# Two split matmuls per unit, and the q/k weights 128 bytes further on

## The chip, the cores and the metric

The kernel runs on one core of one Trainium2 chip. The metric is the device time of one execution in microseconds (us), as the median of several runs. The time of the kernel before is 1561.7 us, the median of three runs.

## The reference, cut to what matters

One decoder layer over a sequence of 512 tokens with model width 2048, all in float32:

```python
xn = _rmsnorm(h, norm_w)
proj = jnp.einsum('bsd,de->bse', xn, w_in)
q, k, v_m, o_m, z_m, i_pre, f_pre, u_g, v_g, z_g = _split_cols(proj)
qk = silu(_causal_depthwise_conv(concat([q, k]), conv_w, conv_b))
hm = _mlstm_chunkwise(q, k, v, log_i, log_f)          # 8 heads, causal
y_m = rmsnorm_per_head(hm) * mlstm_norm_w * sigmoid(o_m) * silu(z_m)
vg = layernorm(gelu(v_g)); sv = einsum('hts,bnshc->bnthc', w_s, vg) + b_spatial
y_g = gelu(u_g) * sv * silu(z_g)
h = h + einsum('bse,ed->bsd', concat([y_m, y_g]), w_out)
return _rmsnorm(h, final_norm_w)
```

Almost all of the arithmetic is the two large products: 512 x 2048 by 2048 x 14352, and 512 x 4096 by 4096 x 2048.

## The kernel before, in words

**Arithmetic.** Each float32 operand is split in two parts of the matmul type float32r: a high part `h`, made by ScalarE as a cast (lines 176 and 186), and the remainder `l`, made by VectorE as a subtraction (lines 177 and 187). A product is the sum of three matmuls, high by high, high by low and low by high. A matmul instruction consists of a weight load of 128 columns (the profile's engine PEld) and the pass of the moving operand (the profile's engine PE).

**Units and chunks.** The input projection is cut in 28 units in a fixed order (`unit_order`, line 40). The first is done with plain products of 512 columns. Each of the other 27 runs through 8 chunks of the contraction and uses a Strassen-like scheme with 7 products in place of 8 (`PRODUCTS`, line 32; `products`, line 785). So a chunk has 7 products x 2 halves t x 3 matmuls = 42 matmuls of 256 columns, and a unit 336. Of each chunk 5 blocks of weights are loaded (640 KB, queue of SyncE, line 150), a second DMA on GpSimd's queue adds two of them in place (line 151), and lines 183 to 187 form the sums and split all 7 blocks into `wh` and `wl`. Chunk n is multiplied while chunk n + 2 is split and chunk n + 4 is loaded (lines 806 to 808). There are three buffers each for `wh` and `wl`, and four for the raw weights `wf`.

**Two kinds of units.** In most units ("token units": vv, oz, uz, v) the stationary operand is a slice of 128 tokens of x, and the moving operand a block of 256 weight columns. In the four units qk the roles are swapped (line 794): the stationary operand is a weight slice, the moving one is x.

**After a unit**, `combine` (line 367) adds the seven accumulators with ScalarE and VectorE, and the rest of the unit's work (activations, the mixing matmul of line 455, the transposes of line 473, the convolution of q and k) is put into a queue `bg`, from which three pieces are taken after each chunk (line 814). So in the third and fourth chunk of the unit behind a uz unit, two groups of four matmuls of line 455 and two groups of four transposes of line 473 stand among the 42 matmuls of a chunk.

**The second half** of the kernel is the output projection. Its part "g" uses plain products of 512 columns (lines 853 to 855), with the eight mLSTM heads in the background, from a shared pool `tp` of twelve temporary buffers of 2 KB. Its part "m" uses `products` again, 4 column groups of 6 chunks (line 876), always in the token roles. A last part does the remaining rows with lines 917 to 919 and the final norm.

**Placement.** The pools stand one behind another in each partition of the on-chip memory, in the order of lines 54 to 61. `gap` and `gap2` hold only spacers, of `GAP_X` and `GAP_W` float32 elements (lines 105 and 106), so they set the byte offset between the pool `xa` (x, 16 buffers of 3072 bytes), `xb` (more of x, 16 buffers of 4096 bytes) and `wp` (the weights). Weights of plain products stand `OFF` = 16 elements (64 bytes) into their buffers (lines 155 and 174); those of all Strassen units stand at offset 0 (lines 180 and 181).

Of the kernel before, what the change touches and what calls it, by code (L numbers as in the profile page):

```python
# [16 lines left out]
P = 128  # L17
D = 2048
S = 512
H = 256  # L20
# [12 lines left out]
    ("q1", 0, 1), ("q6", 4, 5), ("q2", 1, 0), ("q7", 3, 4), ("q5", 6, 3), ("q4", 2, 6), ("q3", 5, 2),  # L33
]
WS = 7 * H
OFF = 16
GAP_X, GAP_W = 24, 112


def unit_order():  # L40
# [7 lines left out]
def hybrid_layer(ctx, tc, xs, x, w_first, w_mid, w_gate, w_out, w_last, par, bif, ws_t, sgu, fin_w, out):  # L48
# [30 lines left out]
    for w in range(9):  # L79
# [13 lines left out]
    nc.gpsimd.memset(ones, 1.0)  # L93
    mhalf = one.tile([P, 8], F32, name="mhalf")
    nc.gpsimd.memset(mhalf, -0.5)
    mask = one.tile([P, P], F32, name="mask")
    nc.gpsimd.memset(mask, 0.0)
    nc.gpsimd.affine_select(
        out=mask, in_=mask, pattern=[[1, P]], compare_op=ALU.is_ge,
        fill=BIG, base=0, channel_multiplier=-1,  # L100
    )
    r_tok = one.tile([P, NT], F32, name="r_tok")
    r_b = one.tile([P, S], F32, name="r_b")
    gst = one.tile([P, 14, NH], F32, name="gst")
# [14 lines left out]
    chunks = []  # L119
    for un in range(NA):  # L120
        for j in range(NP):
            chunks.append(("std", w_first[j]) if un == 0 else ("str", w_mid[un - 1, j]))
    NB0 = len(chunks)
    b_chunks = []
    for kind in "gm":
# [26 lines left out]

    def split_first(a):
        if 0 not in splits:
            splits[0] = tuple(wp.tile([P, WS], F32R, tag=tag, name=f"{tag}0", bufs=3)[:, OFF:OFF + 1024].rearrange(
                "p (a b) -> p a b", a=2) for tag in ("wh", "wl"))
        h, l = splits[0]
        f = raws[0][:, a * S:(a + 1) * S]
        nc.scalar.copy(h[:, a, :], f)
        nc.vector.tensor_tensor(l[:, a, :], f, h[:, a, :].bitcast(F32), op=ALU.subtract)  # L160

    def split(n):
        if n >= NCH or n in splits:
            return
        kind = chunks[n][0]
        t = raws[n]
        raws[n] = None
        if kind == "std":
            if n >= NF0 + 2:
                h = xb.tile([P, 2, S], F32R, tag="xb", name=f"fh{n}")  # L170
                l = xb.tile([P, 2, S], F32R, tag="xb", name=f"fl{n}")
            else:
                h, l = (wp.tile([P, WS], F32R, tag=tag, name=f"{tag}{n}", bufs=bufs)[
                    :, OFF:OFF + 1024].rearrange("p (a b) -> p a b", a=2) for tag, bufs in (("wh", 3), ("wl", 3)))
            f = t[:, 0:1024].rearrange("p (a b) -> p a b", a=2)
            nc.scalar.copy(h, f)  # L176
            nc.vector.tensor_tensor(l, f, h.bitcast(F32), op=ALU.subtract)  # L177
            splits[n] = (h, l)
            return
        h = wp.tile([P, WS], F32R, tag="wh", name=f"wh{n}", bufs=3)  # L180
        l = wp.tile([P, WS], F32R, tag="wl", name=f"wl{n}", bufs=3)
        e = wp.tile([P, 2 * H], F32, tag="we", name=f"we{n}", bufs=1)
        nc.vector.tensor_tensor(e[:, 0:H], t[:, 3 * H:4 * H], t[:, 2 * H:3 * H], op=ALU.add)  # L183
        nc.vector.tensor_tensor(e[:, H:2 * H], e[:, 0:H], t[:, 0:H], op=ALU.add)  # L184
        for f, c in ((t, slice(0, 5 * H)), (e, slice(5 * H, WS))):
            nc.scalar.copy(h[:, c], f)  # L186
            nc.vector.tensor_tensor(l[:, c], f, h[:, c].bitcast(F32), op=ALU.subtract)  # L187
        splits[n] = tuple(v.rearrange("p (a b) -> p a b", a=7) for v in (h, l))
# [58 lines left out]
            nc.scalar.activation(t, t, AF.Square, accum_out=ssq8[:, tt, c:c + 1])  # L247

    def stats_end():
        ssq = sm.tile([P, NT], F32, tag="s4", name="ssq", bufs=8)  # L250
        nc.vector.reduce_sum(ssq, ssq8, axis=mybir.AxisListType.X)
        nc.vector.tensor_scalar(ssq, ssq, 1.0 / D, EPS, op0=ALU.mult, op1=ALU.add)
        nc.gpsimd.tensor_tensor(r_tok, ssq, mhalf[:, :NT], op=ALU.pow)
# [307 lines left out]
    def st_s(h, s0):  # L561
        w = S - s0 * P
        (qh, ql), (kh, kl) = qk_t[h]
        ks = slice(s0 * P, (s0 + 1) * P)
        wm = max(w, H)
        ps_ = bank(f"s{h}_{s0}")
        nc.tensor.matmul(ps_[:, 0:wm], lhsT=kh[:, ks], rhs=qh[:, S - wm:], start=True, stop=False)
        nc.tensor.matmul(ps_[:, 0:wm], lhsT=kh[:, ks], rhs=ql[:, S - wm:], start=False, stop=False)
        nc.tensor.matmul(ps_[:, 0:wm], lhsT=kl[:, ks], rhs=qh[:, S - wm:], start=False, stop=True)
        ps = ps_[:, wm - w:wm]  # L570
        pt = temp(f"p{h}_{s0}")
        cb = cb_t[h]
        g = gst[:, pair(s0, s0), h:h + 1]
        nc.vector.scalar_tensor_tensor(pt[:, 0:P], in0=cb[:, s0 * P:(s0 + 1) * P], scalar=g, in1=mask,
                                       op0=ALU.subtract, op1=ALU.max)
        nc.scalar.activation(pt[:, 0:P], pt[:, 0:P], AF.Exp, scale=-1.0)
        for t0 in range(s0 + 1, NT):
            nc.scalar.activation(pt[:, (t0 - s0) * P:(t0 - s0 + 1) * P], cb[:, t0 * P:(t0 + 1) * P], AF.Exp,
                                 scale=-1.0, bias=gst[:, pair(s0, t0), h:h + 1])
        nc.vector.scalar_tensor_tensor(pt[:, 0:w], in0=ps[:, 0:w], scalar=float(P) ** -0.5, in1=pt[:, 0:w],  # L580
                                       op0=ALU.mult, op1=ALU.mult)
        if s0 == 0:
            hi, lo = (xa.tile([P, 3 * H], F32R, tag="xa", name=f"s{c}{h}_0")[:, 0:S] for c in "hl")
        elif s0 == 1:
            t = xa.tile([P, 3 * H], F32R, tag="xa", name=f"s{h}_1")
            hi, lo = t[:, 0:w], t[:, w:2 * w]
        else:
            if s0 == 2:
                sp_t[(h, "t")] = xa.tile([P, 3 * H], F32R, tag="xa", name=f"s{h}_2")
            t = sp_t[(h, "t")][:, (0 if s0 == 2 else 512):]  # L590
            hi, lo = t[:, 0:w], t[:, w:2 * w]
        nc.scalar.copy(hi, pt[:, 0:w])
        nc.vector.tensor_tensor(lo, pt[:, 0:w], hi.bitcast(F32), op=ALU.subtract)
        sp_t[(h, s0)] = (hi, lo)
# [17 lines left out]
    def st_norm(h):  # L612
        oz_t[h] = []
        for a in range(2):
            t = half(f"oz{h}_{a}")
            nc.gpsimd.dma_start(t, oz_dram[h][:, 2 * a:2 * a + 2, :])
            oz_t[h].append(t)
        ht = h_t[h]
        da = sm.tile([P, NT], F32, tag="s4", name=f"da{h}", bufs=8)
        nc.vector.scalar_tensor_tensor(da, in0=den_t[h], scalar=-1.0, in1=den_t[h], op0=ALU.mult, op1=ALU.max)  # L620
        nc.vector.tensor_tensor(da, da, gst[:, 10:14, h], op=ALU.max)
        rr = sm.tile([P, NT], F32, tag="s4", name=f"rr{h}", bufs=8)
        nc.vector.reciprocal(rr, da)
        ssq = sm.tile([P, NT], F32, tag="s4", name=f"sq{h}", bufs=8)
        junk = temp(f"jk{h}")[:, 0:H]
        for t0 in range(NT):
            nc.scalar.activation(junk, ht[t0 // 2][:, t0 % 2, 0:H], AF.Square, scale=rr[:, t0:t0 + 1],
                                 accum_out=ssq[:, t0:t0 + 1])
        nc.vector.tensor_scalar(ssq, ssq, 1.0 / H, EPS, op0=ALU.mult, op1=ALU.add)
        rn = sm.tile([P, NT], F32, tag="s4", name=f"rn{h}", bufs=8)  # L630
        nc.gpsimd.tensor_tensor(rn, ssq, mhalf[:, :NT], op=ALU.pow)
        hc = sm.tile([P, NT], F32, tag="hc", name=f"hc{h}", bufs=4)
        nc.vector.tensor_tensor(hc, rr, rn, op=ALU.mult)
        hc_t[h] = hc
# [83 lines left out]
        while tag not in done:  # L718
            bg.popleft()()

    act_warm = sm.tile([P, 8], F32, tag="aw", name="act_warm", bufs=1)
    nc.scalar.copy(act_warm, mhalf)

    load_x(0)
# [57 lines left out]
        return {name: (pp if p < 4 else pm).tile([P, S], F32, tag="p" if p < 4 else "m", name=f"{name}_{un}")  # L782
                for p, (name, _, _) in enumerate(PRODUCTS)}

    def products(q, xj, wh, wl, opening, closing, features):
        for name, xsl, wsl in PRODUCTS:
            xh, xl = xj[xsl]
            ps = q[name]
            for t in range(2):
                o = ps[:, t * H:(t + 1) * H]  # L790
                cs = slice(t * P, (t + 1) * P)
                first, last = opening and t == 0, closing and t == 1
                if features:
# [1 line left out]
                else:  # L795
                    ops = ((xh[:, cs], wh[:, wsl, :]), (xh[:, cs], wl[:, wsl, :]), (xl[:, cs], wh[:, wsl, :]))
                for a, (st_, mv_) in enumerate(ops):
                    nc.tensor.matmul(o, lhsT=st_, rhs=mv_, start=(first and a == 0), stop=(last and a == 2),  # L798
                                     skip_group_check=True)

    for un in range(1, NA):
        kind, i = order[un]
        q = product_banks(un)
        for j in range(NP):
            n = un * NP + j
            load(n + 4)
            split(n + 2)
            products(q, X[j], *splits.pop(n), j == 0, j == NP - 1, kind == "qk")
            if j == NP - 1:
                c = combine(un, q)  # L810
                AFTER[kind](i, c)
            if un == NA - 1 and j >= 1:
                load_y("g", j - 1)
            run_bg(3)
    while bg:
        run_bg(1)
    load_y("g", NP - 1)
    bg.append(gates)
    queue_loads(0)
    bg.extend([pause] * 6)  # L820
    bg.append(gate_shifts)
# [13 lines left out]
    for m, (kind, dq, g) in enumerate(b_chunks):  # L835
# [31 lines left out]
        else:  # L867
            if g == 0:
                q = product_banks(f"m{dq}")
                res = {}  # L870
                for a in range(2):
                    for b in range(2):
                        t = half(f"xc{dq}_{a}{b}")
                        nc.sync.dma_start(t, block(acc_dram, a, b, dq))
                        res[(a, b)] = t
            products(q, Y[("m", g)], wh, wl, g == 0, g == 5, False)
            if g == 5:
                c = combine(f"m{dq}", q)
                for a in range(2):
# [142 lines left out]
```

## Time and profile before

| | |
|---|---|
| median of 3 runs | 1561.7 us (1553.22 to 1561.98) |
| profiled execution, its own time | 1571.57 us |
| span of the profiled execution, first to last instruction | 1569.9 us |
| mean granted TensorE clock | 0.997 |
| matmuls / weight loads | 11864 / 11864 |

The profile is one execution recorded by the hardware. A row of the timeline gives the start of an instruction in us from the span's start, its duration, engine, line of the kernel, output and inputs by name, and shape. A duration there includes a pipeline latency, so matmuls overlap in it: how fast they follow one another is read from the differences of their starts. A row of the table of windows gives a stretch of time and, for each engine, its busy time and in brackets how many instructions had a part in the stretch.

### The profile page before, as it was taken

To read this page: it belongs to the slowest core of one execution; us is meant where nothing else is said; L and a number is where in the kernel's file an instruction comes from. 1 tells how busy PE (TensorE), PEld (TensorE's weight loads), DVE (VectorE), ACT (ScalarE), POOL (GpSimd) and SP (SyncE) were. 2 spreads that over 40 slices of the span, in tenths; PEclk is the share of its full clock that TensorE was granted. 3 is DMA by queue.
4 is the path that set the end of the run, shared out by engine and by line. 5 is a ranking of instruction groups with operands and counts; after the bars stand their busy time and mean duration, and the time that the engine had idled before them with its cause. 6 is when DMAs were issued, how large, how long until landed. Compare 5 with 4: busy or idle time off the path is not lost. (4 is left out here: it accounts for less than half of the span.)

```text
span 1569.9 us, 30095 instructions
## 1 busy us (share of the span) xinstructions
PE 1545.9 (98%) x11864; PEld 1485.4 (95%) x11864; DVE 1183.7 (75%) x1944; ACT 874.6 (56%) x1340; POOL 285.3 (18%) x384
## 2 busy tenths in 40 slices
PE   9999999999999999999999999999999999999997
PEld 7899999999999999999999999999988788889986
DVE  8787767877966876976877977678887665697875
ACT  6665455654654555554655565454776666553333
POOL 1411112211122211121211111111202222011100
PEclk9999999999999999999999999999999999999999
DMA  9777878787788777778787777877964665798962
GB/s 319 210 192 187 228 177 209 185 202 193 213 203 215 188 211 184 210 190 214 192 211 186 200 203 199 212 201 196 277 195 156 206 226 188 238 265 238 277 231 107
DMA packets 118510, 326.99 MB, mean 208 GB/s; under 512 B 13534, under 2 KB 20702, under 8 KB 118369
## 3 DMA queue, kind: packets, MB, share of 16 engines
q1 hardware_dynamic: 77456, 243.30, 48.1%
q0 software_dynamic: 40192, 80.66, 26.7%
q8 instruction: 93, 1.52, 0.4%
q10 hardware_dynamic: 720, 1.11, 0.2%
q14 instruction: 49, 0.39, 0.1%
HBM read 229.37 MB, written 32.74 MB: 167 GB/s over the span
## 5 line engine op out<-in xcount | busy, mean ns | idle before, releaser
L186 ACT CAST wh<-wf 128x1280 fp32r<-128x1280 f32 x240 | 301.9, 1264 | 379.9 <-issue 237.8
L187 DVE TENSOR_TENSOR wl<-wf,wh 128x1280 fp32r<-128x1280 f32 x240 | 356.7, 1488 | 174.3 <-ACT wh L186 174.0
L798 PE MATMUL q<-wh,xbh 128*128 128x256 f32 x1472 | 413.7, 281 | 1.4 <-ACT e L774 1.4
L798 PE MATMUL q<-wl,xbh 128*128 128x256 f32 x1472 | 412.9, 281 | 1.2 <-DVE wl L187 1.2
L798 PE MATMUL q<-wh,xbl 128*128 128x256 f32 x1472 | 412.7, 280 | 0.0
L151 POOL DMA_DIRECT2D wf<-wf x240 | 205.3, 857 | 1010.9 <-DMA wf<-w_mid 243.2
L798 PE MATMUL q<-wh,xah 128*128 128x256 f32 x1104 | 311.8, 282 | 0.0
L798 PE MATMUL q<-wl,xah 128*128 128x256 f32 x1104 | 309.5, 280 | 0.0
L798 PE MATMUL q<-wh,xal 128*128 128x256 f32 x1104 | 309.4, 280 | 0.0
L798 PEld LDWEIGHTS q<-wh,xbh 128*128 128x128 f32 x1472 | 281.1, 191 | 1.8 <-ACT e L774 1.6
L798 PEld LDWEIGHTS q<-wl,xbh 128*128 128x128 f32 x1472 | 276.9, 188 | 1.9 <-DVE wl L187 1.8
L798 PEld LDWEIGHTS q<-wh,xbl 128*128 128x128 f32 x1472 | 276.3, 188 | 0.0
L798 PEld LDWEIGHTS q<-wh,xah 128*128 128x128 f32 x1104 | 210.8, 191 | 0.7 <-ACT e L774 0.2
L798 PEld LDWEIGHTS q<-wl,xah 128*128 128x128 f32 x1104 | 207.7, 188 | 0.1
L798 PEld LDWEIGHTS q<-wh,xal 128*128 128x128 f32 x1104 | 207.2, 188 | 0.0
L186 ACT CAST wh<-we 128x512 fp32r<-128x512 f32 x240 | 148.2, 618 | 89.6 <-DVE we L184 89.2
L187 DVE TENSOR_TENSOR wl<-we,wh 128x512 fp32r<-128x512 f32 x240 | 164.7, 686 | 17.2 <-ACT wh L186 17.2
L183 DVE TENSOR_TENSOR we<-wf 128x256 f32<-128x256 f32 x240 | 101.4, 422 | 20.0 <-issue 9.0
L184 DVE TENSOR_TENSOR we<-we,wf 128x256 f32<-128x256 f32 x240 | 101.4, 423 | 5.4
L853 PE MATMUL og<-wh,ygh 128*128 128x512 f32 x256 | 100.9, 396 | 1.6 <-ACT wh L176 1.6
L854 PE MATMUL og<-wl,ygh 128*128 128x512 f32 x256 | 101.5, 397 | 0.1
L855 PE MATMUL og<-wh,ygl 128*128 128x512 f32 x256 | 101.3, 396 | 0.0
(284 smaller groups left out, 2865.9 us busy)
## 6 DMA issues: line engine op xcount, KB each, us to landing
wf<-w_mid SPq DMA_DIRECT2D x216, 640.0 KB, 4.7
wf<-wf POOLq DMA_DIRECT2D x240, 256.0 KB, 5.2
wf<-w_out_p SPq DMA_DIRECT2D x40, 512.0 KB, 4.1
wf<-w_last SPq DMA_DIRECT2D x24, 640.0 KB, 5.7
xr<-xs SPq DMA_DIRECT2D x16, 256.0 KB, 6.1
xt<-x SPq DMA_DIRECT2D x8, 512.0 KB, 7.5
ozd<-e SPq DMA_DIRECT2D x16, 256.0 KB, 2.6
ygd<-yfg SPq DMA_DIRECT2D x16, 256.0 KB, 4.5
```

What stands on the lines that cost most here:

```text
L151: nc.gpsimd.dma_start(t[:, 3 * H:5 * H], t[:, H:3 * H], accum_op=ALU.add)
L183: nc.vector.tensor_tensor(e[:, 0:H], t[:, 3 * H:4 * H], t[:, 2 * H:3 * H], op=ALU.add)
L184: nc.vector.tensor_tensor(e[:, H:2 * H], e[:, 0:H], t[:, 0:H], op=ALU.add)
L186: nc.scalar.copy(h[:, c], f)
L187: nc.vector.tensor_tensor(l[:, c], f, h[:, c].bitcast(F32), op=ALU.subtract)
L798: nc.tensor.matmul(o, lhsT=st_, rhs=mv_, start=(first and a == 0), stop=(last and a == 2), skip_group_check=True)
L853: nc.tensor.matmul(acc[q], lhsT=yh[:, kk, cs], rhs=wh[:, kk, :], start=st, stop=False)
L854: nc.tensor.matmul(acc[q], lhsT=yh[:, kk, cs], rhs=wl[:, kk, :], start=False, stop=False)
L855: nc.tensor.matmul(acc[q], lhsT=yl[:, kk, cs], rhs=wh[:, kk, :], start=False, stop=sp_)
```

## The change

It has three parts.

1. **Two cuts per unit.** In each of the 27 Strassen units, one of the 42 matmuls of chunk 0 (product q3, second half, first of three) and one of chunk 4 (product q1, second half, first of three) is issued as two matmuls of 128 columns, each with the same stationary operand and its own weight load. In the part "m" the same is done in chunks 1 and 3 of each of the four column groups (product q1). That makes 27 x 2 + 4 x 2 = 62 matmuls more. The sums are the same.
2. **Placement.** The weight buffers get 64 elements (256 bytes) longer. In the qk units the weights stand 128 bytes into the buffer (`OFF_FEAT`); in the token units they stay at 0. The spacers shrink from 24 to 16 and from 112 to 48 elements.
3. **Small tiles.** The triangular mask (512 bytes, made at the start) becomes a buffer of the pool `tp`, made by GpSimd at the beginning of part "g" through the queue `bg`, and kept for all heads; small tiles of tag s4 go from 8 to 6 buffers; a scratch tile moves into `tp`.

```diff
 WS = 7 * H
-OFF = 16
-GAP_X, GAP_W = 24, 112
+WSLOT = WS + 64
+OFF, OFF_TOK, OFF_FEAT = 16, 0, 32
+GAP_X, GAP_W = 16, 48
...
-    mask = one.tile([P, P], F32, name="mask")
-    nc.gpsimd.memset(mask, 0.0)
-    nc.gpsimd.affine_select(out=mask, in_=mask, ...)
+    masks = []
+    def make_mask():
+        mask = temp("mask")[:, 0:P]
+        nc.gpsimd.memset(mask, 0.0)
+        nc.gpsimd.affine_select(out=mask, in_=mask, ...)
+        masks.append(mask)
...
-            chunks.append(("std", w_first[j]) if un == 0 else ("str", w_mid[un - 1, j]))
+            chunks.append(("std", w_first[j]) if un == 0 else
+                          ("strf" if order[un][0] == "qk" else "str", w_mid[un - 1, j]))
...
-        h = wp.tile([P, WS], F32R, tag="wh", name=f"wh{n}", bufs=3)
-        l = wp.tile([P, WS], F32R, tag="wl", name=f"wl{n}", bufs=3)
+        o = OFF_FEAT if kind == "strf" else OFF_TOK
+        h, l = (wp.tile([P, WSLOT], F32R, tag=tag, name=f"{tag}{n}", bufs=3)[:, o:o + WS] for tag in ("wh", "wl"))
...
-                    nc.tensor.matmul(o, lhsT=st_, rhs=mv_, start=(first and a == 0), stop=(last and a == 2),
-                                     skip_group_check=True)
+                    parts = (0, P, H) if (name, t, a) == cut else (0, H)
+                    for c0, c1 in zip(parts, parts[1:]):
+                        nc.tensor.matmul(ps[:, t * H + c0:t * H + c1], lhsT=st_, rhs=mv_[:, c0:c1],
+                                         start=(first and a == 0), stop=(last and a == 2), skip_group_check=True)
...
-            products(q, X[j], *splits.pop(n), j == 0, j == NP - 1, kind == "qk")
+            cut = {0: ("q3", 1, 0), 4: ("q1", 1, 0)}.get(j)
+            products(q, X[j], *splits.pop(n), j == 0, j == NP - 1, kind == "qk", cut)
...
     bg.append(gates)
+    bg.append(make_mask)
...
-            products(q, Y[("m", g)], wh, wl, g == 0, g == 5, False)
+            products(q, Y[("m", g)], wh, wl, g == 0, g == 5, False, ("q1", 1, 0) if g in (1, 3) else None)
```

More of the change, by code (lines that the diff above doesn't have):

```diff
@@ L95, in hybrid_layer @@
     nc.gpsimd.memset(mhalf, -0.5)
-    mask = one.tile([P, P], F32, name="mask")
-    nc.gpsimd.memset(mask, 0.0)
[L98 to L101, printed above, removed]
+    masks = []
+    def make_mask():
+        mask = temp("mask")[:, 0:P]
+        nc.gpsimd.memset(mask, 0.0)
+        nc.gpsimd.affine_select(
+            out=mask, in_=mask, pattern=[[1, P]], compare_op=ALU.is_ge,
+            fill=BIG, base=0, channel_multiplier=-1,
+        )
+        masks.append(mask)
     r_tok = one.tile([P, NT], F32, name="r_tok")
@@ L154, in split_first @@
         if 0 not in splits:
-            splits[0] = tuple(wp.tile([P, WS], F32R, tag=tag, name=f"{tag}0", bufs=3)[:, OFF:OFF + 1024].rearrange(
+            splits[0] = tuple(wp.tile([P, WSLOT], F32R, tag=tag, name=f"{tag}0", bufs=3)[:, OFF:OFF + 1024].rearrange(
                 "p (a b) -> p a b", a=2) for tag in ("wh", "wl"))
@@ L172, in split @@
             else:
-                h, l = (wp.tile([P, WS], F32R, tag=tag, name=f"{tag}{n}", bufs=bufs)[
+                h, l = (wp.tile([P, WSLOT], F32R, tag=tag, name=f"{tag}{n}", bufs=bufs)[
                     :, OFF:OFF + 1024].rearrange("p (a b) -> p a b", a=2) for tag, bufs in (("wh", 3), ("wl", 3)))
@@ L249, in stats_end @@
     def stats_end():
-        ssq = sm.tile([P, NT], F32, tag="s4", name="ssq", bufs=8)
+        ssq = sm.tile([P, NT], F32, tag="s4", name="ssq", bufs=6)
         nc.vector.reduce_sum(ssq, ssq8, axis=mybir.AxisListType.X)
@@ L573, in st_s @@
         g = gst[:, pair(s0, s0), h:h + 1]
-        nc.vector.scalar_tensor_tensor(pt[:, 0:P], in0=cb[:, s0 * P:(s0 + 1) * P], scalar=g, in1=mask,
+        nc.vector.scalar_tensor_tensor(pt[:, 0:P], in0=cb[:, s0 * P:(s0 + 1) * P], scalar=g, in1=masks[0],
                                        op0=ALU.subtract, op1=ALU.max)
@@ L618, in st_norm @@
         ht = h_t[h]
-        da = sm.tile([P, NT], F32, tag="s4", name=f"da{h}", bufs=8)
+        da = sm.tile([P, NT], F32, tag="s4", name=f"da{h}", bufs=6)
         nc.vector.scalar_tensor_tensor(da, in0=den_t[h], scalar=-1.0, in1=den_t[h], op0=ALU.mult, op1=ALU.max)
         nc.vector.tensor_tensor(da, da, gst[:, 10:14, h], op=ALU.max)
-        rr = sm.tile([P, NT], F32, tag="s4", name=f"rr{h}", bufs=8)
+        rr = sm.tile([P, NT], F32, tag="s4", name=f"rr{h}", bufs=6)
         nc.vector.reciprocal(rr, da)
-        ssq = sm.tile([P, NT], F32, tag="s4", name=f"sq{h}", bufs=8)
+        ssq = sm.tile([P, NT], F32, tag="s4", name=f"sq{h}", bufs=6)
         junk = temp(f"jk{h}")[:, 0:H]
@@ L629, in st_norm @@
         nc.vector.tensor_scalar(ssq, ssq, 1.0 / H, EPS, op0=ALU.mult, op1=ALU.add)
-        rn = sm.tile([P, NT], F32, tag="s4", name=f"rn{h}", bufs=8)
+        rn = sm.tile([P, NT], F32, tag="s4", name=f"rn{h}", bufs=6)
         nc.gpsimd.tensor_tensor(rn, ssq, mhalf[:, :NT], op=ALU.pow)
@@ L719, in flush @@
             bg.popleft()()
-    act_warm = sm.tile([P, 8], F32, tag="aw", name="act_warm", bufs=1)
+    act_warm = temp("act_warm")[:, 0:8]
     nc.scalar.copy(act_warm, mhalf)
@@ L783, in product_banks, with products @@
                 for p, (name, _, _) in enumerate(PRODUCTS)}
-    def products(q, xj, wh, wl, opening, closing, features):
+    def products(q, xj, wh, wl, opening, closing, features, cut=None):
         for name, xsl, wsl in PRODUCTS:
@@ L789, in products @@
             for t in range(2):
-                o = ps[:, t * H:(t + 1) * H]
                 cs = slice(t * P, (t + 1) * P)
```

## The prediction, made before the changed kernel was run

> **What bounds the kernel now.** I read the page first: the span, the share of each engine, the largest groups.
>
> ```profile
> span 1569.9 us, 30095 instructions
> ...
> PE 1545.9 (98%) x11864; PEld 1485.4 (95%) x11864; DVE 1183.7 (75%) x1944; ACT 874.6 (56%) x1340; POOL 285.3 (18%) x384
> ...
> L798 PE MATMUL q<-wh,xbh 128*128 128x256 f32 x1472 | 413.7, 281 | 1.4 <-ACT e L774 1.4
> L798 PE MATMUL q<-wl,xbh 128*128 128x256 f32 x1472 | 412.9, 281 | 1.2 <-DVE wl L187 1.2
> ```
>
> PE is busy for 98% of the span, and line 798, the Strassen matmul, is most of it: 30 x 336 = 10,080 of the 11,864 matmuls. Next the waits of PE up to 1150 us, and one line of all waits.
>
> ```profile
> PE q L798 <- ACT e L774: 1.4, 1, 1.4
> PE p L760 <- ACT wh L159: 1.3, 1, 1.3
> PE q L798 <- DVE wl L187: 1.2, 3, 0.8
> ```
>
> ```profile
> ACT wh L186 <- PE q L798: 94.5, 46, 3.2
> ```
>
> PE waits for next to nothing. ScalarE waits 94.5 us for PE to give back a weight buffer, so the splits run ahead of PE. Only what PE itself takes per matmul can move the time much. The mean of 281 ns in the page is overlapped and hides that; the starts in the timeline show it. Here are the first and the last row of two stretches, of 161 and 155 matmuls in unbroken sequence:
>
> ```profile
> 389.77 0.28 PE L798 MATMUL q<-wh,xah 128*128 128x256 f32 x1
> ...
> 407.90 0.28 PE L798 MATMUL q<-wl,xah 128*128 128x256 f32 x1
> ```
>
> ```profile
> 1052.78 0.28 PE L798 MATMUL q<-xah,wh 128*128 128x256 f32 x1
> ...
> 1070.91 0.28 PE L798 MATMUL q<-xbl,wh 128*128 128x256 f32 x1
> ```
>
> 18.13 us / 160 = **113.3 ns** in the first, 18.13 / 154 = **117.7 ns** in the second. Instruction, shape and clock are the same; there are two paces, 4.4 ns apart. The table of windows, matmuls of line 798 alone, shows where each holds (the count includes two or three that overlap an edge):
>
> ```profile
> 104.00:144.00 40.00, 40.00 (x342) 1.00 0.75 201
> 630.00:670.00 40.00, 40.00 (x342) 1.00 0.80 214
> 1440.00:1470.00 30.00, 30.00 (x257) 1.00 0.97 272
> 388.60:437.00 48.40, 47.85 (x420) 1.00 0.76 205
> 1073.80:1116.00 42.20, 41.97 (x367) 1.00 0.79 213
> ```
>
> (342 - 2) / 40 us is 117.6 ns, and 117.6 again in the part "m" at 1440. The fast pace holds in the last two windows and in some short stretches. Counted over all starts of line 798, about 1,060 matmuls run at the fast and 8,920 at the slow pace; the rest has a break before or after it. How a stretch becomes fast or slow is in the timeline:
>
> ```profile
> 156.73 0.81 PE L455 MATMUL mx<-e,ws 128*128 128x256 f32 x3
> 157.19 0.47 PE L798 MATMUL q<-wh,xbh 128*128 128x256 f32 x1
> 157.50 0.28 PE L798 MATMUL q<-wl,xbh 128*128 128x256 f32 x1
> 157.62 0.28 PE L798 MATMUL q<-wh,xbl 128*128 128x256 f32 x1
> 157.74 0.28 PE L798 MATMUL q<-wh,xah 128*128 128x256 f32 x1
> ...
> 158.19 0.28 PE L798 MATMUL q<-wl,xah 128*128 128x256 f32 x1
> ```
>
> ```profile
> 161.14 0.66 PE L473 MATMUL ytg<-ident,e 128*128 128x128 f32 x4
> 161.56 0.36 PE L798 MATMUL q<-wh,xah 128*128 128x256 f32 x1
> 161.76 0.28 PE L798 MATMUL q<-wl,xah 128*128 128x256 f32 x1
> ...
> 162.93 0.28 PE L798 MATMUL q<-wh,xbl 128*128 128x256 f32 x1
> ```
>
> After the mixing matmuls four intervals take 0.45 us (113 ns); after the second group of transposes, ten take 1.17 us (117). This repeats in all token units that hold these groups: fast after line 455, slow after the second group of line 473, and then it stays, for up to 1,280 matmuls. So the pace is a phase between weight loads and moving passes: it keeps itself up, and a short foreign instruction can shift it. In the qk units, where the two operands swap places, the same mixing matmuls do not help. First and last of the 18 matmuls between two groups of line 455:
>
> ```profile
> 355.86 1.02 PE L455 MATMUL mx<-e,ws 128*128 128x256 f32 x4
> ...
> 357.78 0.28 PE L798 MATMUL q<-xbh,wh 128*128 128x256 f32 x1
> ...
> 359.79 0.28 PE L798 MATMUL q<-xbh,wl 128*128 128x256 f32 x1
> ```
>
> 2.01 / 17 = 118 ns. No matmul sequence in the four qk units is fast.
>
> **Why the placement can matter.** `xa`, `xb` and the weights consist of buffers and slices that are multiples of 256 bytes. The first weight buffer stands 16 x 3072 + 16 x 4096 + 448 bytes behind the first x buffer, which is 192 modulo 256. So stationary minus moving address is 64 modulo 256 in token units and 192 in qk units. After the change the spacer is 192 instead of 448 bytes: again 192 modulo 256, so token units keep their 64. With 128 bytes more, a qk unit gets 192 + 128 = 64 as well. If the phase depends on this residue, qk units become like token units. That the period is 256 bytes is an assumption; that the swap matters is seen.
>
> **The change part by part**, against the profiled execution's own 1571.57 us, 0.6% above the median of 1561.7.
>
> - *Slow matmuls made fast.* The first cut comes with the last product of chunk 0, when a unit has taken all its accumulators, the second at the start of chunk 4, just behind the last transposes. If each cut leaves the fast phase, as the short groups of line 455 do, 8,920 x (117.7 - 113.3) = **-39.7 us** (4.45 unrounded). Bounds: 0, if a cut leaves the phase as it was, to -39.7.
> - *Left slow.* Chunk 3 behind the transposes up to the second cut, some 34 matmuls in each of eight units, and the starts before the first cuts: 450 x 4.4 ns = **+2.0**.
> - *The cuts themselves.* 62 more weight loads and passes. No row shows a float32r matmul of 128 columns; the nearest is the transposes of 128 columns, four of which take 161.14 to 161.56, 105 ns each. The halves have as many columns together as the whole, so the lower bound is 0; the upper is a whole slow interval, 118 ns. I take 105: **+6.5** (0 to 7.3). TensorE: Matmul & The Clock Gate in the Trainium skill, section LDWEIGHTS, puts a load of 128 columns at 107 ns; by it the term would be an estimated +6.6.
> - *Settling.* The two intervals behind 157.50 are 0.12 instead of 0.113, and with rounding I allow 0.02 us per cut: **+1.2**.
> - *VectorE.* At the fast pace a unit takes 38.1 us in place of 39.6. The heaviest units for VectorE are those behind a qk unit:
>
> ```profile
> 389.00:427.00 38.00, 37.81 (x334) 37.61 (x333) 36.11 (x59) 21.05 (x26) 6.20 (x8) 1.00 0.78 212
> 588.00:629.00 41.00, 40.97 (x342) 40.55 (x342) 28.57 (x41) 22.97 (x30) 6.53 (x8) 1.00 0.73 185
> ```
>
> The first is fast already, with VectorE (fourth column) busy for 36.11 of 38 us, and the other, a typical one, needs 28.57. So VectorE keeps up on the whole, with short waits in seven heavy units, of the size of the three above (1.2 us together, 0.8 the longest): **+2.3** (0 to 5.6).
> - *Part "m"* at 1440 has its DMA engines busy for 0.97 of the time and may not follow a faster pace: its 1,008 matmuls are worth 4.5 us, I take **+1** (0 to 4.5).
> - *Mask in the pool.* Part "g" has 11 instead of 12 buffers for everything else. Its fills are on GpSimd:
>
> ```profile
> L98 POOL TENSOR_SCALAR_AFFINE_SELECT mask<-mask 128x128 f32<-128x128 f32 x1 | 0.5, 497 | 0.0
> ```
>
> ```profile
> 1227.17 1.66 PE L473 MATMUL ytm<-ident,oz 128*128 128x128 f32 x4 [2.51 <-DVE oz L639]
> 1228.48 0.77 PE L853 MATMUL og<-wh,ygh 128*128 128x512 f32 x1
> 1229.06 0.63 PE L854 MATMUL og<-wl,ygh 128*128 128x512 f32 x1
> ```
>
> The fill stands on GpSimd's queue ahead of the first head's DMAs, which are six chunks early; 0.5 us there is hidden. A missing buffer would show as one more wait like that of 2.51 us. I take one, less what is hidden: **+2** (0 to 20, one for each of eight heads). Fewer s4 buffers and the moved scratch tile cost 0: a head uses four s4 tiles and six are left.
>
> Sum: -39.7 + 2.0 + 6.5 + 1.2 + 2.3 + 1 + 2 = **-24.7 us**; 1571.57 - 24.7 = 1546.9 for a profiled execution. Scaled by 1561.7 / 1571.57 that is **1537 us**.
>
> **The rivals.** *Half an effect.* The residue matters modulo 512, not 256. The new weight buffer of 7424 bytes is 14.5 x 512, so every other buffer would stand wrong, or the fast phase does not last from one cut to the next. For it: the phase did flip within units. Against it: it lasted over unit borders (388.6 to 437). Half of the gain with the cuts paid: -19.9 + 6.5 + 1.2 + 2 = -10, 1552 us.
>
> *Nothing happens.* Two cuts and an offset do not shift the phase: +6.5 + 2 = +8.5, 1570 us. For it: the stop of 1.4 us at the first unit ended slow too, so not every disturbance helps. Against it: line 455 always did. SBUF — State Buffer in the Trainium skill, section Who interferes with whom, speaks for this rival: TensorE has independent read ports for moving operand and weight load and never waits for anyone, so an address could not matter. The trace disagrees in part, with 113.3 and 117.7 ns for one instruction; what causes it no row shows.
>
> *The cut sets the slow phase*, as the second group of 128-column transposes always does (161.14). The place is each cut; from the first on, the 1,060 fast matmuls are lost too: 1,060 x 4.45 ns = +4.7, with the cuts +6.5 and the mask +2 it is +13.2, 1575 us, slower. It decides if the interval behind a cut is 118 ns and stays so.
>
> **How the numbers follow.** The forecast has a chance of 0.62, half an effect 0.14, nothing 0.13, slower 0.11. The forecast's own range is 1526 (cuts free, no new waits) to 1549 (qk units stay slow, 4 x 336 x 4.45 ns = 6 us, and more waits on the pool). To leave out no more than 2 in 10, the range must take in half an effect and reach towards nothing with cheap cuts: **1524 to 1567**. A measurement can tell about 1% from no change, that is under 1546 or over 1577. The forecast is below that but for 0.04, half an effect mostly above: faster 0.62, same 0.32, slower 0.06.
>
> **What would show it.** Right: windows of 40 us in the token units hold about 355 matmuls of line 798 in place of 342, those of the qk units too; behind the cut in chunk 4 the interval falls from 118 to 113 ns within some five matmuls; there are 11,926 matmuls. Wrong: 118 ns behind the cuts (then the phase was not theirs to set); fast token units but slow qk units (then the residue isn't the rule); fast pace with the gain lost in waits of PE for `wl` of line 187, for `wf`, or in part "g" for a temporary buffer.

## The result, and the profile after

| | kernel before | changed kernel |
|---|---|---|
| median of 16 runs | 1562.53 us | 1551.95 us |
| lowest to highest | 1553.22 to 1571.74 | 1548.60 to 1559.74 |
| ratio, 95% interval | | 0.9929 (0.9910 to 0.9948) |
| profiled execution, its own time | 1571.57 us | 1551.84 us |

The change makes the kernel faster by 0.7%, 10.6 us, where 24.7 us were forecast. Between the two profiled executions the difference is 19.7 us. These two numbers, 10.6 and 19.7, are the first thing to explain. One run of the changed kernel, in its repetition below, took 3090.84 us, twice the others; its ratio leaves it out, and nothing here shows why. The page of the changed kernel:

```profile
span 1550.1 us, 30205 instructions
...
PE 1522.6 (98%) x11926; PEld 1461.1 (94%) x11926; DVE 1182.3 (76%) x1944; ACT 876.1 (57%) x1340; POOL 279.0 (18%) x384
...
L806 PE MATMUL q<-wh,xbh 128*128 128x256 f32 (+1 forms) x1495 | 409.5, 276 | 1.4 <-ACT e L781 1.4
L806 PE MATMUL q<-wl,xbh 128*128 128x256 f32 x1472 | 409.9, 278 | 1.0 <-DVE wl L194 1.0
```

Line 806 is what line 798 was. PE stays the bound, with 62 instructions more and 23 us less of busy time. The means fell from 281 to 276 and 278 ns. The waits of PE up to 1150 us, and ScalarE's wait for PE:

```profile
PE q L806 <- DVE wl L194: 1.0, 3, 0.3
```

```profile
ACT wh L193 <- PE q L806: 114.0, 50, 3.3
```

So the splits still run ahead. The windows that were read before, for line 806:

```profile
104.00:144.00 40.00, 40.00 (x355) 1.00 0.81 213
630.00:670.00 40.00, 39.55 (x345) 1.00 0.82 211
1440.00:1470.00 30.00, 29.84 (x259) 1.00 0.95 263
```

The first has 355 matmuls where there were 342. The second has 345, since a stop and a group of transposes now fall into it. The third, in part "m", has 259 in place of 257, although 221 of its matmuls run at the fast pace: two cuts and, at the border between two column groups, short stops of 0.8 us together fall into it. And a cut that starts from the slow pace, the second of the first Strassen unit (the row with x2 is the cut matmul):

```profile
85.02 0.28 PE L806 MATMUL q<-wh,xah 128*128 128x256 f32 x1
85.13 0.28 PE L806 MATMUL q<-wl,xah 128*128 128x256 f32 x1
85.25 0.28 PE L806 MATMUL q<-wh,xal 128*128 128x256 f32 x1
85.37 0.33 PE L806 MATMUL q<-wh,xah 128*128 128x128 f32 x2
85.54 0.34 PE L806 MATMUL q<-wl,xah 128*128 128x256 f32 x1
...
86.19 0.28 PE L806 MATMUL q<-wh,xbh 128*128 128x256 f32 x1
...
87.43 0.28 PE L806 MATMUL q<-wh,xbl 128*128 128x256 f32 x1
```

From 86.19 to 87.43 are eleven intervals of 113 ns: slow before the cut, fast behind it. Counted over all starts, 8,394 matmuls of line 806 run at 113.3 and 1,365 at 117.8 ns; in the profile of before it was 1,058 and 8,921. Below, "slow" is this number of matmuls at the slow pace.

### The profile page after: what moved, and what is told of

It is laid out like the page before. It is cut to its first block, busy times and chain, and to the rows that moved or that the text cites. A ratio compares the mean times of both kernels' runs of the same rounds, so it can differ in the third digit from the quotient of the medians.

```text
span 1550.1 us, 30205 instructions
## 1 busy us (share of the span) xinstructions
PE 1522.6 (98%) x11926; PEld 1461.1 (94%) x11926; DVE 1182.3 (76%) x1944; ACT 876.1 (57%) x1340; POOL 279.0 (18%) x384
## 5 line engine op out<-in xcount | busy, mean ns | idle before, releaser
L806 PE MATMUL q<-wh,xbh 128*128 128x256 f32 (+1 forms) x1495 | 409.5, 276 | 1.4 <-ACT e L781 1.4
L806 PE MATMUL q<-wh,xbl 128*128 128x256 f32 x1472 | 407.2, 277 | 0.0
L806 PE MATMUL q<-wh,xah 128*128 128x256 f32 (+1 forms) x1127 | 308.0, 277 | 0.4 <-DVE e L380 0.4
L806 PE MATMUL q<-wh,xal 128*128 128x256 f32 x1104 | 305.4, 277 | 0.0
```

Of the source, the lines that this page charges most:

```text
L806: nc.tensor.matmul(ps[:, t * H + c0:t * H + c1], lhsT=st_, rhs=mv_[:, c0:c1], start=(first and a == 0), stop=(last and a == 2), skip_group ...
```

## The experiments

### The same kernel again

Three more profiles of the kernel before, to see whether the one that was read is typical. No edit.

> The unchanged kernel before, profiled once more. Theory A (the share of fast matmuls differs from execution to execution, and the profile of before on which the prediction was built caught a slow one): this execution's own time lies nearer the median of 1562.5 us, and its number of slow matmuls of line 798 is lower than 8,921 by 225 for each us that it is below 1571.6, so some 6,900 at 1562.5 us. Theory B (profiling itself, or another stage, made those 9 us): about 1571 us again with about 8,920 slow matmuls, or a lower time with the same 8,920.

> The same kernel a third time, for a third point. Theory A: time and number of slow matmuls again lie on one line of 4.4 ns per slow matmul, wherever the time falls. Theory B: no such line.

> The kernel before, profiled a fourth time. Theory A (time follows the share of fast matmuls, which differs from execution to execution): if the time is near the median of 1562 us, 6,000 to 7,500 slow matmuls; near 1553 us, 4,000 to 5,000; near 1571 us, 7,800 to 9,000. It falls if a time under 1556 us comes with over 7,500 slow ones, or one over 1568 us with fewer than 6,000.

| execution of the kernel before | its time | slow in all | slow in the input projection | time of these units |
|---|---|---|---|---|
| the one that the prediction read | 1571.57 us | 8,921 | 7,918 | 1092.6 us |
| second | 1552.32 us | 4,142 | 3,898 | 1077.0 us |
| third | 1571.79 us | 7,848 | 7,618 | 1095.3 us |
| fourth | 1564.52 us | 5,874 | 5,619 | 1085.7 us |

The second execution, in the windows of 104 and 1030 us; the latter lies in the last qk unit:

```profile
104.00:144.00 40.00, 40.00 (x356) 1.00 0.79 204
...
1030.00:1060.00 30.00, 30.00 (x266) 1.00 0.85 222
```

356 matmuls in 40 us and 266 in 30 us are the fast pace, without any cut, and in a qk unit on the old placement too. So the share of fast matmuls differs from one execution to the next, from a tenth to more than half, and the time goes with it. In the units of the input projection (line 798 up to the first matmul of part "g") the four executions lie on one line of 4.4 ns per slow matmul within about 2 us: from 3,898 to 7,918 it would be +17.8 us and was +15.6. Over the whole kernel the line is less clean. The third execution has 1,073 slow matmuls fewer than the first and the same time. Of these, 773 are in part "m", worth 3.4 us, and it became only 1.3 us shorter, since its stops grew from 0.5 to 2.6 us. The fourth has 5,874 where I expected 6,000 or more. Theory B (profiling makes the 9 us) falls with the second execution: profiled, and 1552.32 us.

### Each part of the change alone

The changed kernel without cuts:

```diff
-            cut = {0: ("q3", 1, 0), 4: ("q1", 1, 0)}.get(j)
+            cut = None
...
-            products(q, Y[("m", g)], wh, wl, g == 0, g == 5, False, ("q1", 1, 0) if g in (1, 3) else None)
+            products(q, Y[("m", g)], wh, wl, g == 0, g == 5, False, None)
```

> The changed kernel without any cut, so placement, mask and small tiles alone. Theory A (cuts set the phase, the residue of 64 bytes lets it last): token units as in the kernel before, mostly slow after the second transposes, but the qk units can now be fast, also after line 462's mixing matmuls; some 300 to 1,500 slow matmuls fewer, ratio 0.995 to 1.003. Rival (the placement alone does it): nearly all matmuls fast and a ratio of 0.990 or lower, since the cuts' cost is saved too.

The kernel before with the cuts alone, on the old placement, the mask where it was:

```diff
+                    parts = (0, P, H) if (name, t, a) == cut else (0, H)
+                    for c0, c1 in zip(parts, parts[1:]):
...
+            cut = {0: ("q3", 1, 0), 4: ("q1", 1, 0)}.get(j)
...
```

> The kernel before with the 62 cuts alone, on the old placement. Theory A: token units and the part m fast nearly throughout, the four qk units slow (1,344 matmuls at 118 ns), ratio 0.993 to 0.998: the changed kernel's gain less 4 x 336 x 4.4 ns = 6 us, plus some 3 us if the mask in the pool cost that in part g. Rival (cuts work only with the new placement): token units slow behind the cuts, ratio 1.000 to 1.006.

| | median | ratio to before, interval | slow |
|---|---|---|---|
| placement alone | 1566.06 us | 1.0015 (0.9991 to 1.0038) | 5,502 |
| cuts alone | 1550.26 us | 0.9923 (0.9893 to 0.9953) | 1,589 |
| both (changed kernel) | 1551.95 us | 0.9929 (0.9910 to 0.9948) | 1,365 |

The cuts do all of it. Placement alone is not faster, and its number of slow matmuls is one that the kernel before has too. Its four qk units, which I had expected could be fast now, were slow for 231 to 336 of their 336 matmuls. I had expected the qk units to be slow throughout with cuts alone, and they are not. The first three have 241 slow matmuls each (110 in the changed kernel), and the fourth, in which no transposes stand, has none. So the new placement saves 3 x 131 x 4.4 ns = 1.7 us there, too little to show in the ratios.

### What the residue decides

The changed kernel with the two offsets exchanged, so that stationary minus moving address is 192 modulo 256 in all Strassen units:

```diff
-OFF, OFF_TOK, OFF_FEAT = 16, 0, 32
+OFF, OFF_TOK, OFF_FEAT = 16, 32, 0
```

> The changed kernel with the two offsets exchanged: token weights 128 bytes on, q and k weights at 0, so that stationary minus moving address is 192 modulo 256 in every Strassen unit. Theory C (the residue does not decide whether a fast phase can last, only what a disturbance leaves behind): units without disturbances fast from the first cut on, 1,400 to 3,000 slow matmuls, 1550 to 1558 us. Theory D (64 is needed, as the prediction had it): token units slow behind every cut, over 7,000 slow matmuls, 1570 us or more.

1569.03 us, ratio 1.0017 (0.9994 to 1.0040), 5,775 slow: between what the two theories gave. Its first cut in chunk 0 of the second unit:

```profile
108.83 0.28 PE L806 MATMUL q<-wh,xbh 128*128 128x256 f32 x1
108.95 0.28 PE L806 MATMUL q<-wl,xbh 128*128 128x256 f32 x1
109.07 0.28 PE L806 MATMUL q<-wh,xbl 128*128 128x256 f32 x1
109.19 0.33 PE L806 MATMUL q<-wh,xbh 128*128 128x128 f32 x2
109.36 0.33 PE L806 MATMUL q<-wl,xbh 128*128 128x256 f32 x1
109.53 0.28 PE L806 MATMUL q<-wh,xbl 128*128 128x256 f32 x1
...
110.24 0.28 PE L806 MATMUL q<-wh,xal 128*128 128x256 f32 x1
```

From 109.53 to 110.24 are six intervals of 118 ns: slow before the cut, slow behind it. The same cut in the changed kernel, which comes from the fast pace:

```profile
108.51 0.28 PE L806 MATMUL q<-wh,xbl 128*128 128x256 f32 x1
108.62 0.33 PE L806 MATMUL q<-wh,xbh 128*128 128x128 f32 x2
108.79 0.33 PE L806 MATMUL q<-wl,xbh 128*128 128x256 f32 x1
108.96 0.28 PE L806 MATMUL q<-wh,xbl 128*128 128x256 f32 x1
109.08 0.28 PE L806 MATMUL q<-wh,xah 128*128 128x256 f32 x1
109.20 0.28 PE L806 MATMUL q<-wl,xah 128*128 128x256 f32 x1
109.32 0.28 PE L806 MATMUL q<-wh,xal 128*128 128x256 f32 x1
109.43 0.28 PE L806 MATMUL q<-wh,xah 128*128 128x256 f32 x1
...
109.77 0.28 PE L806 MATMUL q<-wh,xbh 128*128 128x256 f32 x1
```

Here the phase is first pushed (0.12 us each from 108.96 to 109.32) and settles at 113 ns from 109.43 on. In the exchanged kernel a cut from the fast pace is followed by 113 ns at once, and two of the first fourteen cuts did turn a slow stretch fast; the others left what they found. Counted over all 62 cuts of each kernel, by the pace ahead of a cut and the pace from the ninth matmul behind it on:

| | from fast: stays fast, turns slow | from slow: turns fast, stays slow |
|---|---|---|
| changed kernel, 64 | 43, 3 | 16, 0 |
| exchanged offsets, 192 | 19, 0 | 9, 34 |

In the three cases that turn slow, a stop of PE or other matmuls follow within five instructions. So at 64 a cut leads to the fast pace from either side, and at 192 it mostly keeps the one that it meets. It is not the place of the weights alone, nor the role of the operands: in the changed kernel cuts turn slow stretches in token units (weights at 0, 7 of 7) and in qk units (weights 128 bytes on, 7 of 7), in the exchanged one in 7 of 31 token cases (128 on) and none of 8 in qk units (at 0). Both paces can last at both residues. Theory D, the prediction's assumption, falls as worded, since fast stretches last at 192. Theory C holds in its mechanism alone: the count is about twice what I had given it, and the time, 1569 us for 1550 to 1558, was missed too.

The cuts on the old kernel with the weights at residue 0 (the plain products keep theirs):

```diff
-OFF = 16
-GAP_X, GAP_W = 24, 112
+OFF = 0
+GAP_X, GAP_W = 24, 64
```

> The cuts on the placement of before, with the spacer ahead of the weights set so that the difference of addresses is 0 modulo 256 in Strassen units (it stays 0 in plain products). If a fast phase exists only at some residues, 0 should show another pace, such as 118 ns throughout, about 1575 us; if the residue hardly matters, again about 1,500 slow matmuls and 1548 to 1556 us.

```profile
104.00:144.00 40.00, 40.00 (x336) 1.00 0.77 196
```

1599.48 us in one run, above both expectations. There is a third pace, **120.0 ns**, in nearly all matmuls (336 in 40 us), and no cut leads away from it. Against the cuts alone on the old placement, 1550.26 us, the moved weights cost 49 us, although no instruction changes. The starts show where: in all three paces a weight load starts about 3 ns behind the matmul ahead of it, and its own matmul starts 110 ns after it at the fast pace, 114 to 116 at the slow one and 117 to 118 here. What takes these 4 to 8 ns is not shown. Nor is 0 the slowest residue for every shape: the plain products of 512 columns in part "g" stand at 0 in all these kernels and mostly follow one another every 226 or 227 ns, twice 113.3.

### The cut itself

Cutting after 64 columns instead of 128:

```diff
-                    parts = (0, P, H) if (name, t, a) == cut else (0, H)
+                    parts = (0, 64, H) if (name, t, a) == cut else (0, H)
```

> The cuts on the placement of before, but after 64 columns of 256 and not after 128. If any short pass with a weight load of its own sets the fast phase, 1,300 to 1,900 slow matmuls and 1548 to 1554 us, as with 128 columns; if it needs half a pass, the interval behind the cuts stays 118 ns and the time is over 1565 us.

1554.48 us in one run, 1,720 slow. Half a pass is not needed:

```profile
83.55 0.36 PE L799 MATMUL q<-wh,xah 128*128 128x64 f32 x2
83.75 0.31 PE L799 MATMUL q<-wl,xah 128*128 128x256 f32 x1
83.89 0.28 PE L799 MATMUL q<-wh,xal 128*128 128x256 f32 x1
...
84.36 0.28 PE L799 MATMUL q<-wh,xbh 128*128 128x256 f32 x1
84.47 0.28 PE L799 MATMUL q<-wl,xbh 128*128 128x256 f32 x1
84.58 0.28 PE L799 MATMUL q<-wh,xbl 128*128 128x256 f32 x1
```

The cuts in every chunk, 240 in place of 62:

```diff
-            cut = {0: ("q3", 1, 0), 4: ("q1", 1, 0)}.get(j)
+            cut = ("q3", 1, 0) if j == 0 else ("q1", 1, 0)
...
```

> The cuts on the placement of before, in every chunk: 240 in place of 62. By what the cuts cost in the profile of the changed kernel, 57 ns each and some 15 ns of settling, 178 more are +12.8 us; they take back about half of the 1,525 slow matmuls and more, -3 to -5 us: 1556 to 1562 us. By the price of the prediction, 105 ns and 20, it would be +22 us less 4, 1566 to 1570 us.

1572.66 us in one run, 22.4 us over the kernel with 62 cuts, though only 1,020 matmuls are slow. The price of 57 ns in my expectation was a misreading; it counted only the two halves, 58 + 112 ns in place of 113. The rows from 108.62 to 109.43 above show the rest: the cut matmul and the five behind it take 0.81 us, where six fast ones take 6 x 113.3 = 680 ns, so a cut costs about 130 ns. From the unrounded starts it is 58 + 112 + 170 + 118 + 119 + 116 + 114 = 807 ns, **127 ns** more: one whole fast interval of 113, and 14 of settling. The other 37 cuts of the changed kernel that are met and left at the fast pace, without a stop, cost 127 ns each as well. 178 more cuts are +22.6 us by that, less 569 x 4.4 ns = 2.5 for fewer slow matmuls: +20.1, measured +22.4.

### The mask

The profiles show part "g" (first matmul of "g" to first of "m") at 244.3 us in the changed kernel, 242.3 in placement alone and 245.5 in the exchanged one, which all have the mask in the pool; without it, at 237 to 242 in eight profiles. In the next two kernels the mask is written over the tile of ones, which is free by then. The second also has 28 instead of 54 cuts in the input projection. The changed kernel ran on the same chip once more.

```diff
-        mask = temp("mask")[:, 0:P]
+        mask = ones
```

> The changed kernel as it is, on the same chip as the next two. About 1552 us and some 1,365 slow matmuls, ratio 0.991 to 0.995, part g about 244 us.

> The changed kernel, but the mask is written over the tile of ones, which nobody reads after the gates, and so takes no buffer of the temporary pool. Theory E (the mask in the pool costs about 4 us in part g, where the profiles with it show 242 to 246 us and those without it 237 to 242): part g 238 to 241 us and 3 to 5 us off the changed kernel's time, about 1548 us. Rival (those differences are chance between executions): the same time as the changed kernel within 2 us.

> As the kernel with the mask in the tile of ones, with 28 cuts in place of 54 in the units of the input projection: in chunk 0 only where operands change roles or a heavy unit for VectorE went before, in chunk 4 only behind a uz unit. If a cut costs a whole weight load and its settling, 127 ns, 26 fewer are -3.3 us, less what is slow for longer after a stop, 0 to 1.5 us: 1545 to 1547 us. If the phase is lost more often than the cuts kept here can mend, slow matmuls go from 1,365 to over 2,500 and it is slower, 1552 us.

| | median | ratio to before, interval | part "g" | slow |
|---|---|---|---|---|
| changed kernel again | 1553.30 us | 0.9952 (0.9933 to 0.9972) | 244.1 us | 924 |
| mask over ones | 1548.13 us | 0.9932 (0.9914 to 0.9951) | 239.6 us | 1,220 |
| mask over ones, fewer cuts | 1548.26 us | 0.9933 (0.9913 to 0.9953) | 235.9 us | 1,097 |

Part "g" begins and ends in the changed kernel and in the one with the mask over ones at

```profile
1133.20 0.39 PE L863 MATMUL og<-wh,ygh 128*128 128x512 f32 x1
...
1377.46 0.28 PE L806 MATMUL q_m<-wh,ybh 128*128 128x256 f32 x1
```

```profile
1134.41 0.39 PE L863 MATMUL og<-wh,ygh 128*128 128x512 f32 x1
...
1374.04 0.28 PE L806 MATMUL q_m<-wh,ybh 128*128 128x256 f32 x1
```

244.3 against 239.6 us. The waits of PE in these stretches show the difference, first in the changed kernel, then with the mask over ones:

```profile
PE ytm L480 <- DVE p L587: 5.8, 3, 2.9
```

```profile
PE ytm L480 <- DVE p L587: 1.3, 2, 0.9
```

These are the transposes of line 480 behind VectorE's work on a temporary buffer `p`; the two kernels differ in the mask's buffer alone. The wait takes 5.0 to 7.3 us in the four profiles with the mask in the pool, and 0.8 to 1.7 us in the ten without it. By the medians the mask costs 5 us; the intervals of the two ratios overlap, so it is the profiles that carry this, by that wait and by the length of part "g", four with the mask in the pool between 242.3 and 245.5 and ten without between 235.9 and 242.0. The saving from fewer cuts, -3.3 us, did not show: the first Strassen unit stayed slow for 304 of its matmuls, which gives back 1.3 us, and the rest is within what the runs scatter. Both kernels have medians below that of the changed kernel, though not beyond the intervals.

## Why the prediction was right or wrong, point by point

**The bound and the two paces** were right. PE sets the time, the two paces are 113.3 and 117.8 ns, and the cuts bring nearly all matmuls to the fast one.

**The step that failed** is the first term, "8,920 x (117.7 - 113.3) = -39.7 us", with the scaling by 1561.7 / 1571.57 that carried it over to the median. The 8,920 were counted in one execution, and that was one of the slowest that the kernel has: 1571.57 us, where 16 runs go from 1553.22 to 1571.74. The 0.6% between it and the median were not a constant around the span that could be scaled away; to a large part they were the term itself, matmuls that in a median run are fast without any cut. The fourth execution, 1564.52 us, has 5,874 slow matmuls, so (5,874 - 1,365) x 4.44 ns = 20.0 us can be won from it, where the prediction, net of what stays slow, had 37.7. With the cuts' 7.9 us and 3.5 in part "g" against it (244.3 less 240.8 us), 8.6 us are left, near the 10.6 between the medians. The two profiled executions themselves are 12.7 us apart (1564.52 less 1551.84); most of the other 4 us is in the part behind "m", which took 58.5 us in the one and 55.4 in the other, and 55.8 to 58.5 us in the four executions of before. That a median run has about as many slow matmuls as the fourth rests on this one profile. The highest and lowest time of the three runs shown, 1561.98 and 1553.22, were a hint; a spread of 0.6% in a kernel bound by one engine should have been read as a difference in that engine's pace.

**The terms, from profile to profile**, where the same execution of before stands on both sides:

| us | forecast | measured |
|---|---|---|
| slow made fast, net of those left slow | -37.7 | 7,556 x 4.44 ns = -33.5 |
| 62 cuts with settling | +7.7 | 62 x 127 ns = +7.9 |
| waits in the input projection | +2.3 | +1.4 (what is left of its -21.2) |
| part "m" | +1 | +1.1 (what is left of its -1.9) |
| part "g" with the mask in the pool | +2 | +2.3 |
| start and end | 0 | +1.5 and -0.5 |
| sum | -24.7 | -19.8 |

The price of a cut, taken from the transposes as the nearest row, was right in its sum, 124 for 127 ns, with some luck: 105 and 19 were forecast for what was 113 and 14. At 192, a cut between fast matmuls costs 113 to 114 ns and has no settling. More stays slow than the 450 allowed: 1,365, since a stop late in a unit leaves the slow pace until the next cut, and a change of operand roles does too. The mask's +2 is too small against the mean of all profiles, 4 to 5 us; the wait that it adds was of the kind forecast, for VectorE's work in a head. For the waits in the input projection, seven of the mean size that the prediction names, 0.4 us, would have been 2.8 us and not 2.3.

**The placement.** That the residue modulo 256 matters is shown (113.3 or 117.8 ns at 64 and at 192, 120.0 ns at 0). That a qk unit cannot be fast at 192 was wrong: the second execution of before ran a whole one at the fast pace. No sequence of the one profile was fast there, and from that I made a rule. What the 64 gives is that a disturbance ends fast.

**The rivals.** "The cut sets the slow phase" was wrong at 64; at 192 it was half right, since there a cut keeps a slow phase. "Nothing happens" is what the placement alone does. SBUF — State Buffer in the Trainium skill, section Who interferes with whom, gives TensorE two independent read ports and says that it never waits on anyone. That the address could therefore not matter was the prediction's own conclusion, and the 49 us of the kernel at residue 0 are against it; whether the two reads hold each other up is not shown. "Half an effect" gave 1552 us, near the result, by another mechanism: every weight buffer can be fast, so 512 bytes are not the period, and the fast pace lasts through whole units.

## What to carry to other kernels

Before a gain per instruction is multiplied by a count, profile the kernel before more than once: when runs differ by half a per cent, look for what differs in the bounding engine, because part of the gain may be in the median already. A stream of weight loads and moving passes ran at several paces here with the same instructions; look at the differences of starts, and at what comes just ahead of each change of pace. And when a tile is moved into a shared pool to make room, price the buffer that the pool loses.

## What the runs showed of the hardware that was not expected

A pair of weight load and 256-column pass in float32r takes 113.3, 117.8 or 120.0 ns depending on the difference of the two operands' byte addresses modulo 256 (64, 192 and 0 were tried) and, at 64 and 192, on a phase that keeps itself for hundreds of matmuls and came out differently in each of four executions (4,142 to 8,921 slow matmuls in one program). At 64 one short pass is enough to set the fast one, 64 columns as well as 128, at the price of 127 ns. Why the chip does this stays open.
